# A hybrid retention and S5 layer: two small groups of matmuls are laid out on the array's four column groups, in full float

## The chip, the cores and the metric

The kernel runs on one core of one Trainium2 chip. The metric is the device time of one execution in microseconds; the median of three runs counts. A separate, profiled execution gives the rows that are shown: its span goes from the first to the last instruction, and its own time is 2.55 us longer than the span. Engines are named as in the profile: PE is TensorE (matmuls; PEld its loads of weights), DVE is VectorE, ACT is ScalarE, POOL is GpSimd, SP is SyncE, which issues DMAs.

## What is computed

One layer over 1,024 prompt tokens and 8 sample tokens (1,032 columns in all). The normalised input is projected by one wide matrix; the parts feed a retention branch of eight heads and an S5 branch of 64 groups; both are gated, projected, merged and projected again. Two pieces matter here. In retention, the sample rows need a product of the query with the new state, and a normalisation of the result over the head's 128 values:

```python
    q_dec = q * jnp.exp((idx[None, :] + 1.0) * lg[:, None])[None, :, :, None]
    cross = jnp.einsum('bhqd,bhdv->bhqv', q_dec, s0)
...
    mu = jnp.mean(o, axis=-1, keepdims=True)
    var = jnp.mean(jnp.square(o - mu), axis=-1, keepdims=True)
    o = (o - mu) * lax.rsqrt(var + EPS)
```

In S5, each group of 16 channels has a linear recurrence over 64 complex states:

```python
    y = (jnp.einsum('gnp,bcgp->bcgn', cr, xr) - jnp.einsum('gnp,bcgp->bcgn', ci, xi)
         + dsk[None, None] * u_c)
```

## The kernel before, in words

**The large products.** All wide matrices are multiplied by a scheme with seven products for each 2x2 block of tiles; `product` (L924) issues the matmuls of one. Each factor is split into a high and a low half (`fp32r`), and three of the four combinations are summed, so a product is a run of matmuls 256 and 260 columns wide (324 near the end) with weights `whia`, `whib`, `whic` (high) and `wloa`, `wlob`, `wloc` (low). ScalarE casts the high half (L905) and VectorE subtracts it for the low half (`sub`, shown as L85). These products fill TensorE from about 340 us on.

**The branches in between.** The S5 branch and retention are Python generators in a queue `bg`. After each product, `slot()` lets the first of them go on to its next `yield`, with its instructions placed behind the ones just issued. A scheduler then settles the order within each engine; the engines work off their lists in order. So small matmuls of the branches stand in TensorE's list between two products.

**S5.** The 64 groups are handled in 16 blocks of four. `s5_mats` builds `B1` (128 x 4 groups x 16) and `W3` (128 x 4 x 9 x 16); `s5_toep` forms a block's Toeplitz kernels: four float matmuls (L643), with 16 columns of weights each, write 16 partitions x 128 values, side by side along one PSUM bank (`misc`). VectorE copies the bank to `ksb` (L645) and adds the skip term to the first 16 columns, by a multiply of the identity with `dsk` (L647, `dti`) and an addition (L648). Four DMAs from POOL's queue (L650) lay `ksb` out in `t_d` in DRAM as a Toeplitz matrix, and one more (L653) brings it back as `Tm`, for `s5_read` (L720, L721) one block later.

**Retention.** `head` handles one head after the other, eight in all. For the sample rows, VectorE multiplies the new state `s0` by the query (L1141, tile `vT`, 128 x 8 samples x 128), and TensorE sums over the partitions: for each half of the samples, `split` makes a high and a low half in the tile `ktS` (ScalarE, then VectorE), and eight matmuls (L1149) with an 8-column selector `sel` add row b of an 8 x 128 result. The two halves are one `yield`, so one product, apart. The result goes to `ons` (8 x 128, L1153), is normalised with the prompt's chunks (L1165 to L1179, with powers on GpSimd, L1171 and L1172), and is transposed by an 8-row transpose (L1190) behind the last group of full transposes (L1185). `load_vk` (L1064) loads the next head's `vT` from POOL's queue.

PSUM in this stretch: three double banks `acc` for the products and two single banks `misc` for all the rest.

Of the kernel before, what the change touches and what calls it, by code (L numbers as in the profile page):

```python
# [48 lines left out]
def constants():  # L49
# [25 lines left out]
    c["sgn"] = sg  # L75
    c["sel"] = np.ascontiguousarray(np.broadcast_to(np.eye(8, dtype=f).reshape(1, 64), (128, 64)))
    return c


def emit(ctx, tc, I, O):  # L80
# [6 lines left out]
    def mul(out, a, b, eng=None):  # L87
        tt(out, a, b, ALU.mult, eng)
# [310 lines left out]
    def s5_params():  # L399
# [9 lines left out]
        A.dma_start(prm, I["prm"])  # L409
        dsk = s5q.tile([16, G], F32, name="dsk")  # L410
        A.dma_start(dsk, I["dsk"])
        pp["dsk"] = dsk
        lr, li, ld = prm[:, 0, :], prm[:, 1, :], prm[:, 2, :]
# [220 lines left out]
    def s5_toep(b):  # L634
        g0 = 4 * b
        pp = s5p
        d = s5d[b]
        B1, W3 = d["B1"], d["W3"]
        U = d["U"] = W("U", [128, 4, 144])
        P.dma_start(U, ub_d[g0 * 16:g0 * 16 + 64].rearrange("(g n) s c -> (n s) g c", g=4))  # L640
        ps = misc()
        for g in range(4):
            T.matmul(ps[0:16, g * 128:(g + 1) * 128], B1[:, g, :], W3[:, g, 0:8, :], start=True, stop=True)  # L643
# [395 lines left out]
    def ret_const():  # L1039
# [17 lines left out]
        V.tensor_copy(K["sel"], selr.rearrange("p (b c) -> p b c", b=8))  # L1057
        yield
# [10 lines left out]
    def head(h):  # L1069
# [74 lines left out]
        for i in range(2):  # L1144
            hl = R("ktS", [128, 2, 4, 128], 1, F32R)
            split((hl[:, 0], hl[:, 1]), pq[:, 4 * i:4 * i + 4])
            for b in range(4):
                for e in range(2):
                    T.matmul(ps[0:8, 0:128], sel[:, 4 * i + b, :], hl[:, e, b, :], start=i + b + e == 0, stop=i == 1 and b == 3 and e == 1)  # L1149
# [13 lines left out]
        if h != HEADS[-1]:  # L1163
            K["next"] = load_vk(HEADS[HEADS.index(h) + 1])
        V.bn_stats(bn[0:8, 8], ons)  # L1165
        V.bn_aggr(mv[0:8, 8], bn[0:8, 8])
# [3 lines left out]
        V.tensor_scalar(rs[0:8, 8:9], mv[0:8, 8, 1:2], EPS, None, ALU.add)  # L1170
        P.tensor_tensor(rs[:, 0:8], rs[:, 0:8], mhalf, ALU.pow)  # L1171
        P.tensor_tensor(rs[0:8, 8:9], rs[0:8, 8:9], mhalf[0:8, 0:1], ALU.pow)  # L1172
# [3 lines left out]
        V.scalar_tensor_tensor(nb[0:8, 8:9], mv[0:8, 8, 0:1], -1.0, rs[0:8, 8:9], ALU.mult, ALU.mult)  # L1176
        for n in range(8):
            A.activation(on[:, n], on[:, n], AF.Identity, scale=rs[:, n:n + 1], bias=nb[:, n:n + 1])
        A.activation(ons, ons, AF.Identity, scale=rs[0:8, 8:9], bias=nb[0:8, 8:9])  # L1179
        yield  # L1180
# [8 lines left out]
        ps = misc()  # L1189
        T.transpose(ps[:, 0:8], ons, ident[0:8, 0:8])  # L1190
        mul(oo[:, SEQ:TOK], ps[:, 0:8], za[:, SEQ:TOK])
        P.dma_start(ya_d[h], oo)
# [585 lines left out]
def layouts(i):  # L1778
# [39 lines left out]
    r["x0s"] = c(stack2(xr.transpose(2, 1, 0), xi.transpose(2, 1, 0)))  # L1818
    r["dsk"] = c(a["s5_d"][0].T)
    br, bi = (a[n][0].transpose(1, 0, 2) for n in ("s5_b_re", "s5_b_im"))  # L1820
# [31 lines left out]
```

## Time and profile before

| | us |
|---|---|
| median of three runs | 2562.95 (2561.0 to 2564.02) |
| profiled execution, own time | 2561.65 |
| its span | 2559.1 |
| TensorE busy in it | 2532.5 |
| VectorE / ScalarE / GpSimd busy | 1996.9 / 971.4 / 763.4 |

How to read the rows that follow. A row of the timeline has the start in us from the span's start, the length, the engine, the line, the operation, the tiles (written <- read), the size (for a matmul: rows * columns of weights, then the moving operand) and how many instructions were merged into it; idle time ahead of it stands in brackets, with what ended it. Starts are exact to some hundredths; lengths of matmuls overlap, since they are pipelined. A row of grouped instructions has its busy time and mean length behind the bar, then the idle time ahead. A row of stretches gives, for each engine, busy us and instructions, then TensorE's granted clock (1.00 is full), and DMA share and rate.

### The profile page before, as it was taken

To read this page: it belongs to the slowest core of one execution; us is meant where nothing else is said; L and a number is where in the kernel's file an instruction comes from. 1 tells how busy PE (TensorE), PEld (TensorE's weight loads), DVE (VectorE), ACT (ScalarE), POOL (GpSimd) and SP (SyncE) were. 2 spreads that over 40 slices of the span, in tenths; PEclk is the share of its full clock that TensorE was granted. 3 is DMA by queue.
4 is the path that set the end of the run, shared out by engine and by line. 5 is a ranking of instruction groups with operands and counts; after the bars stand their busy time and mean duration, and the time that the engine had idled before them with its cause. 6 is when DMAs were issued, how large, how long until landed. Compare 5 with 4: busy or idle time off the path is not lost.

```text
span 2559.1 us, 52524 instructions
## 1 busy us (share of the span) xinstructions
PE 2532.5 (99%) x19948; PEld 2486.0 (97%) x19948; DVE 1996.9 (78%) x4183; ACT 971.4 (38%) x1747; POOL 763.4 (30%) x1276
## 2 busy tenths in 40 slices
PE   9999999999999999999999999999999999999998
PEld 8999999999999999999999999999999999999876
DVE  7655988898898887557987667667897878989784
ACT  7113223333233334343334444444552432445532
POOL 0103222222222222333334444434332222433320
PEclk9999999999999999999999999999999999999999
DMA  5886434434444447887879888888888689857884
GB/s 196 262 264 216 156 122 123 134 122 132 129 123 127 124 128 245 199 215 198 209 191 246 231 218 227 202 225 236 275 287 281 222 236 316 296 188 168 212 297 134
DMA packets 233500, 519.09 MB, mean 203 GB/s; under 512 B 33968, under 2 KB 61056, under 8 KB 232480
## 3 DMA queue, kind: packets, MB, share of 16 engines
q0 software_dynamic: 103008, 301.75, 41.7%
q1 hardware_dynamic: 91552, 159.30, 19.8%
q10 hardware_dynamic: 38688, 54.70, 6.7%
q8 instruction: 157, 2.57, 0.4%
q14 instruction: 95, 0.78, 0.1%
HBM read 342.36 MB, written 173.25 MB: 201 GB/s over the span
## 4 chain that ended last, share of the span: by engine, by line
PE 90%; DVE 4%; issue 3%; DMA 2%; POOL 1%; ACT 1%; DVEq 0%; POOLq 0%; ACTq 0%
PE acc L924 71%; PE acc L1755 5%; PE mm L220 3%; PE mm L218 3%; PE mm L219 3%; DVE a L85 1%; PE misc L643 1%; PE misc L721 1%; PE misc L720 1%; PE misc L1135 1%; PE misc L1125 1%; PE misc L1104 1%; DVE u L85 1%; PE misc L671 1%; PE misc L1137 0%
## 5 line engine op out<-in xcount | busy, mean ns | idle before, releaser
L924 PE MATMUL acc<-a,whib 128*128 128x256 f32 (+1 forms) x3656 | 607.0, 285 | 2.3 <-DVE u L85 2.2
L924 PE MATMUL acc<-a,whia 128*128 128x256 f32 (+1 forms) x3656 | 607.2, 285 | 1.7 <-DVE u L85 1.2
L924 PE MATMUL acc<-a,whic 128*128 128x256 f32 (+1 forms) x3664 | 606.9, 285 | 1.2 <-ACT whib L905 0.6
L924 PEld LDWEIGHTS acc<-a,whib 128*128 128x128 f32 x3656 | 508.8, 188 | 6.5 <-ACT whia L905 2.4
L924 PEld LDWEIGHTS acc<-a,whia 128*128 128x128 f32 x3656 | 509.6, 188 | 3.2 <-issue 1.9
L924 PEld LDWEIGHTS acc<-a,whic 128*128 128x128 f32 x3664 | 507.3, 188 | 2.0 <-ACT whib L905 0.8
L924 PE MATMUL acc<-a,wloa 128*128 128x256 f32 (+2 forms) x1828 | 383.4, 284 | 0.0
L924 PE MATMUL acc<-a,wloc 128*128 128x256 f32 (+2 forms) x1832 | 382.8, 283 | 0.4 <-DVE wloc L85 0.4
L924 PE MATMUL acc<-a,wlob 128*128 128x256 f32 (+2 forms) x1828 | 382.8, 284 | 0.0
L924 PEld LDWEIGHTS acc<-a,wloc 128*128 128x128 f32 x1832 | 286.5, 188 | 1.2 <-DVE wloc L85 1.2
L924 PEld LDWEIGHTS acc<-a,wloa 128*128 128x128 f32 x1828 | 286.3, 188 | 0.0
L924 PEld LDWEIGHTS acc<-a,wlob 128*128 128x128 f32 x1828 | 286.0, 188 | 0.2
L905 ACT CAST whib<-wraw 128x512 fp32r<-128x512 f32 x140 | 87.0, 621 | 232.0 <-PE acc L924 181.5
L905 ACT CAST whia<-wraw 128x512 fp32r<-128x512 f32 x142 | 88.1, 620 | 226.8 <-PE acc L924 170.9
L905 ACT CAST whic<-wraw 128x512 fp32r<-128x512 f32 x142 | 88.1, 621 | 213.8 <-PE acc L924 163.2
L85 DVE TENSOR_TENSOR wloa<-wraw,whia 128x512 fp32r<-128x512 f32 x152 | 104.2, 686 | 64.0 <-ACT whia L905 37.3
L85 DVE TENSOR_TENSOR wlob<-wraw,whib 128x512 fp32r<-128x512 f32 x151 | 103.5, 685 | 59.1 <-ACT whib L905 39.4
L85 DVE TENSOR_TENSOR wraw<-wr 128x512 f32<-128x512 f32 x212 | 145.3, 686 | 2.6
L905 ACT CAST whib<-wr 128x512 fp32r<-128x512 f32 x107 | 66.4, 620 | 191.2 <-PE acc L924 169.1
L85 DVE TENSOR_TENSOR wloc<-wraw,whic 128x512 fp32r<-128x512 f32 x153 | 104.8, 685 | 43.8 <-ACT whic L905 29.2
L905 ACT CAST whic<-wr 128x512 fp32r<-128x512 f32 x106 | 65.7, 620 | 190.9 <-PE acc L924 167.8
L905 ACT CAST whia<-wr 128x512 fp32r<-128x512 f32 x105 | 65.1, 620 | 189.3 <-PE acc L924 172.1
(457 smaller groups left out, 4575.8 us busy)
## 6 DMA issues: line engine op xcount, KB each, us to landing
wr<-in_w_in SPq DMA_DIRECT2D x280, 256.0 KB
pt_d<-u POOLq DMA_DIRECT2D x70, 258.0 KB, 3.3
u<-pt_d POOLq DMA_DIRECT2D x70, 258.0 KB, 5.0
wr<-in_w_out SPq DMA_DIRECT2D x64, 256.0 KB
wr<-in_w_outB SPq DMA_DIRECT2D x64, 256.0 KB
stg<-fm_d POOLq DMA_DIRECT2D x44, 258.0 KB, 4.3
pt_d<-st POOLq DMA_DIRECT2D x35, 258.0 KB, 3.3
pt_d<-p POOLq DMA_DIRECT2D x35, 258.0 KB, 2.9
```

The costliest lines, as they stand in the source:

```text
L85: return (eng or V).tensor_tensor(out, a, b, op)
L218: T.matmul(ps, wh[:, i, :], xh[:, t0:t1], start=first, stop=False)
L219: T.matmul(ps, wh[:, i, :], xl[:, t0:t1], start=False, stop=False)
L220: anchor["p"] = T.matmul(ps, wl[:, i, :], xh[:, t0:t1], start=False, stop=last).ins
L643: T.matmul(ps[0:16, g * 128:(g + 1) * 128], B1[:, g, :], W3[:, g, 0:8, :], start=True, stop=True)
L671: T.matmul(ps[:, q * 144:(q + 1) * 144], W1[:, g, :], U[:, g, :], start=True, stop=True)
L720: T.matmul(o, Tm[:, g, :], U[:, g, 0:136], start=True, stop=False)
L721: T.matmul(o, W3[:, g, 1:9, :], X[:, g, 0:136], start=False, stop=True)
L905: anchor["a"] = A.copy(hi, f).ins
L924: anchor["p"] = T.matmul(o, a[:, i, :], x, start=first and i == 0 and a is wh and b is xh, stop=n in (2, 5, 6) and i == 3 and a is wl, ski ...
L1104: T.matmul(ps[:, c * 128:(c + 1) * 128], kt[:, 4 * i + c, :], vt[:, 4 * i + c, :], start=True, stop=True)
L1755: anchor["p"] = T.matmul(ps[c], a, b, start=k == 0 and a is xh and b is wh, stop=k == KD - 1 and a is xl).ins
```

## The change

Both small groups of matmuls get a place in the array (`tile_position`), so that four of them lie on the four groups of 32 columns, in plain float.

The Toeplitz kernel of group g of a block goes to columns 32g to 32g + 31, and so to those partitions of PSUM. Its weights are 32 columns (a pair of groups of `B1`), of whose results 16 rows are used. The bank is then 128 partitions x 128 values instead of 16 x 512; the skip term is added as the first 16 columns are copied, by one operation with two parameters laid out by partition, `dsk` and `eye`. The DMAs to `t_d` have the same sizes and read other partitions.

The sums for samples are taken from the float product itself (`pq`, in `vT`); `split` and its tile go. For each half i, sample 4i + b goes to column group b with a 32-column selector that puts it in row 32b + i. So there are two float matmuls for each column group, one in each half, and the result `ons` has 128 partitions, eight of them used. What handles it (L1153, L1165 to L1179) works on 128 partitions instead of 8; the transpose at the end is a full one, and its multiply picks the eight columns.

```diff
         ps = misc()
         for g in range(4):
-            T.matmul(ps[0:16, g * 128:(g + 1) * 128], B1[:, g, :], W3[:, g, 0:8, :], start=True, stop=True)
-        ksb = W("ksb", [16, 4, 128])
-        V.tensor_copy(ksb, ps[0:16, :].rearrange("p (g l) -> p g l", g=4))
-        dt_ = W("dti", [16, 4, 16])
-        mul(dt_, ident[0:16, 0:16].unsqueeze(1).broadcast_to([16, 4, 16]), pp["dsk"][:, g0:g0 + 4].unsqueeze(2).broadcast_to([16, 4, 16]))
-        add(ksb[:, :, 0:16], ksb[:, :, 0:16], dt_)
+            T.matmul(ps[32 * g:32 * g + 32, 0:128], B1[:, g & 2:(g & 2) + 2, :].rearrange("p g n -> p (g n)"), W3[:, g, 0:8, :],
+                     start=True, stop=True, tile_position=(0, 32 * g))
+        ksb = W("ksb", [128, 128])
+        V.tensor_copy(ksb[:, 16:128], ps[:, 16:128])
+        V.scalar_tensor_tensor(ksb[:, 0:16], pp["eye"], pp["dsk"][:, b:b + 1], ps[:, 0:16], ALU.mult, ALU.add)
         for g in range(4):
             P.dma_start(bass.AP(tensor=t_d.tensor, offset=t_d.offset + (g0 + g) * 32768, ap=[[2048, 16], [272, 8], [1, 128]]),
-                        ksb[:, g, :].unsqueeze(1).broadcast_to([16, 8, 128]))
+                        ksb[32 * g + 16 * (g % 2):32 * g + 16 * (g % 2) + 16].unsqueeze(1).broadcast_to([16, 8, 128]))
...
-        selr = rp.tile([128, 64], F32, name="selr")
-        P.dma_start(selr, I["sel"])
-        K["sel"] = rp.tile([128, 8, 8], F32R, name="sel")
+        K["sel"] = rp.tile([128, 2, 32], F32, name="sel")
+        P.dma_start(K["sel"].rearrange("p b c -> p (b c)"), I["sel"])
...
         ps = misc()
         for i in range(2):
-            hl = R("ktS", [128, 2, 4, 128], 1, F32R)
-            split((hl[:, 0], hl[:, 1]), pq[:, 4 * i:4 * i + 4])
             for b in range(4):
-                for e in range(2):
-                    T.matmul(ps[0:8, 0:128], sel[:, 4 * i + b, :], hl[:, e, b, :], start=i + b + e == 0, stop=i == 1 and b == 3 and e == 1)
+                T.matmul(ps[32 * b:32 * b + 32, 0:128], sel[:, i, :], pq[:, 4 * i + b], start=i == 0, stop=i == 1,
+                         tile_position=(0, 32 * b), skip_group_check=True)
             if i == 0:
                 yield
-        ons = R("ons", [8, 128])
-        A.copy(ons, ps[0:8, 0:128])
+        ons = R("ons", [128, 128])
+        A.copy(ons, ps[:, 0:128])
...
-        P.tensor_tensor(rs[0:8, 8:9], rs[0:8, 8:9], mhalf[0:8, 0:1], ALU.pow)
+        P.tensor_tensor(rs[:, 8:9], rs[:, 8:9], mhalf[:, 0:1], ALU.pow)
...
-        A.activation(ons, ons, AF.Identity, scale=rs[0:8, 8:9], bias=nb[0:8, 8:9])
+        A.activation(ons, ons, AF.Identity, scale=rs[:, 8:9], bias=nb[:, 8:9])
...
         ps = misc()
-        T.transpose(ps[:, 0:8], ons, ident[0:8, 0:8])
-        mul(oo[:, SEQ:TOK], ps[:, 0:8], za[:, SEQ:TOK])
+        T.transpose(ps[:, 0:128], ons, ident)
+        eb = lambda t: t.rearrange("p (e b) -> p e b", e=2)
+        mul(eb(oo[:, SEQ:TOK]), ps[:, 0:128].rearrange("p (b r) -> p r b", r=32)[:, 0:2], eb(za[:, SEQ:TOK]))
```

The order of TensorE's list, at the first sums of the first head; `ktS` holds the split halves, `vT` the product, `acc` the products' banks. Before:

```order
L924 MATMUL acc<-a_2173,wloc 128x256
L924 MATMUL acc<-a_2173,wloc 128x260
L1149 MATMUL misc<-ktS,sel 8x128
L924 MATMUL acc<-a_2233,whia 128x256
L1149 MATMUL misc<-ktS,sel 8x128 x7
L924 MATMUL acc<-a_2233,whia 128x260
```

The same place in the changed kernel, whose line numbers differ by a few:

```order
L923 MATMUL acc<-a_2173,wloc 128x256
L923 MATMUL acc<-a_2173,wloc 128x260
L1143 MATMUL misc<-vT,sel 32x128 x4
L923 MATMUL acc<-a_2233,whia 128x256
L923 MATMUL acc<-a_2233,whia 128x260
```

The eight matmuls with one product matmul among them became four that stand together, at the same place between the same products. The second group (eight, now four), the Toeplitz groups and the transposes also keep their places.

VectorE's list at the same place, from the product with the query on. Before:

```order
L85 TENSOR_TENSOR vT<-a_16965,a_16964 128x1024
L85 TENSOR_TENSOR wlob<-wraw,whib 128x512
L85 TENSOR_TENSOR wraw<-wr,wraw 128x512
L85 TENSOR_TENSOR wraw<-wr 128x512
L85 TENSOR_TENSOR ktS<-vT,ktS 128x512
L85 TENSOR_TENSOR u_17610<-p_17566,acc 128x516
```

And in the changed kernel:

```order
L85 TENSOR_TENSOR vT<-a_16935,a_16934 128x1024
L85 TENSOR_TENSOR wlob<-wraw,whib 128x512
L85 TENSOR_TENSOR wraw<-wr,wraw 128x512
L85 TENSOR_TENSOR wraw<-wr 128x512
L85 TENSOR_TENSOR u_17578<-p_17534,acc 128x516
```

The low half's subtraction, which TensorE's sums read, is gone, and they read what the first row writes.

More of the change, by code (lines that the diff above doesn't have):

```diff
@@ L75, in constants @@
     c["sgn"] = sg
-    c["sel"] = np.ascontiguousarray(np.broadcast_to(np.eye(8, dtype=f).reshape(1, 64), (128, 64)))
+    c["sel"] = np.ascontiguousarray(np.broadcast_to(np.eye(32, dtype=f)[0:2].reshape(1, 64), (128, 64)))
     return c
@@ L409, in s5_params @@
         A.dma_start(prm, I["prm"])
-        dsk = s5q.tile([16, G], F32, name="dsk")
-        A.dma_start(dsk, I["dsk"])
-        pp["dsk"] = dsk
+        for n in ("dsk", "eye"):
+            pp[n] = s5q.tile([128, 16], F32, name=n)
+            A.dma_start(pp[n], I[n])
         lr, li, ld = prm[:, 0, :], prm[:, 1, :], prm[:, 2, :]
@@ L1056, in ret_const @@
         yield
-        V.tensor_copy(K["sel"], selr.rearrange("p (b c) -> p b c", b=8))
         yield
@@ L1164, in head @@
             K["next"] = load_vk(HEADS[HEADS.index(h) + 1])
-        V.bn_stats(bn[0:8, 8], ons)
-        V.bn_aggr(mv[0:8, 8], bn[0:8, 8])
+        V.bn_stats(bn[:, 8], ons)
+        V.bn_aggr(mv[:, 8], bn[:, 8])
         rs = R("rsd", [128, 9])
@@ L1169, in head @@
         V.tensor_scalar(rs[:, 0:8], mv[:, 0:8, 1], col[:, 3, h:h + 1], EPS, ALU.mult, ALU.add)
-        V.tensor_scalar(rs[0:8, 8:9], mv[0:8, 8, 1:2], EPS, None, ALU.add)
+        V.tensor_scalar(rs[:, 8:9], mv[:, 8, 1:2], EPS, None, ALU.add)
         P.tensor_tensor(rs[:, 0:8], rs[:, 0:8], mhalf, ALU.pow)
-        P.tensor_tensor(rs[0:8, 8:9], rs[0:8, 8:9], mhalf[0:8, 0:1], ALU.pow)
+        P.tensor_tensor(rs[:, 8:9], rs[:, 8:9], mhalf[:, 0:1], ALU.pow)
         yield
@@ L1175, in head @@
         V.scalar_tensor_tensor(nb[:, 0:8], mv[:, 0:8, 0], -1.0, rs[:, 0:8], ALU.mult, ALU.mult)
[L1176 removed]
+        V.scalar_tensor_tensor(nb[:, 8:9], mv[:, 8, 0:1], -1.0, rs[:, 8:9], ALU.mult, ALU.mult)
         for n in range(8):
             A.activation(on[:, n], on[:, n], AF.Identity, scale=rs[:, n:n + 1], bias=nb[:, n:n + 1])
[L1179 removed]
+        A.activation(ons, ons, AF.Identity, scale=rs[:, 8:9], bias=nb[:, 8:9])
         yield
@@ L1818, in layouts @@
     r["x0s"] = c(stack2(xr.transpose(2, 1, 0), xi.transpose(2, 1, 0)))
-    r["dsk"] = c(a["s5_d"][0].T)
+    r["dsk"], r["eye"] = np.zeros((4, 32, 16), np.float32), np.zeros((4, 32, 16), np.float32)
+    for g in range(4):
+        rows = slice(16 * (g % 2), 16 * (g % 2) + 16)
+        r["dsk"][g, rows] = a["s5_d"][0].reshape(16, 4, 16)[:, g].T
+        r["eye"][g, rows] = np.eye(16, dtype=np.float32)
+    r["dsk"], r["eye"] = (r[n].reshape(128, 16) for n in ("dsk", "eye"))
     br, bi = (a[n][0].transpose(1, 0, 2) for n in ("s5_b_re", "s5_b_im"))
```

## The prediction

> **What bounds the kernel now.** I read the page first: which engine is busy, and what the chain that ended last is made of.
>
> ```profile
> PE 2532.5 (99%) x19948; PEld 2486.0 (97%) x19948; DVE 1996.9 (78%) x4183; ACT 971.4 (38%) x1747; POOL 763.4 (30%) x1276
> PE 90%; DVE 4%; issue 3%; DMA 2%; POOL 1%; ACT 1%; DVEq 0%; POOLq 0%; ACTq 0%
> ```
>
> Then I asked for the busy time of each engine in the two stretches that the change touches: 340 to 940 us, where the S5 branch is worked off between the products of the large matrices, and 1380 to 1770 us, where retention is.
>
> ```profile
> 340.00:940.00 600.00, 598.76 (x5009) 590.83 (x5008) 532.65 (x1419) 189.63 (x350) 162.85 (x289) 1.00 0.42 126
> 1380.00:1770.00 390.00, 388.62 (x3326) 382.69 (x3325) 265.65 (x598) 176.77 (x339) 160.39 (x236) 1.00 0.84 219
> ```
>
> The first busy figure is TensorE (PE): 598.76 of 600 us and 388.62 of 390. It rests for 1.2 and 1.4 us. So in both stretches TensorE time is kernel time: what a small matmul group takes out of the stream of products is what it costs, and work of the other engines counts only where TensorE waits for it. Busy time can't price a group, since matmuls overlap in it. I price by starts instead, from the timeline: the row ahead of a group, the group, and the rows behind it, until the stream runs at its own pace again. The pace, and one Toeplitz group (L643):
>
> ```profile
> 347.08 0.40 PE L924 MATMUL acc<-a,wloa 128*128 128x256 f32 x2
> 347.32 0.64 PE L924 MATMUL acc<-a,whia 128*128 128x256 f32 x4
> 347.79 0.40 PE L924 MATMUL acc<-a,wloa 128*128 128x256 f32 x2
> 348.12 1.05 PE L643 MATMUL misc<-W,B 128*16 128x128 f32 x8
> 349.10 0.74 PE L924 MATMUL acc<-a,whib 128*128 128x256 f32 x4
> 349.68 0.40 PE L924 MATMUL acc<-a,wlob 128*128 128x256 f32 x2
> ```
>
> Two products take 0.24 us (347.08 to 347.32) and four 0.47 (to 347.79). The group could start at 347.79 + 0.24 = 348.03, and the four products behind it would have begun at 349.68 - 0.47 = 349.21. So it costs 1.18 us. It is four matmuls, each shown as two passes (x8). A group of float matmuls over the full width of the array, for comparison (L1104):
>
> ```profile
> 1360.35 0.40 PE L924 MATMUL acc<-a,wloc 128*128 128x256 f32 x2
> 1360.59 1.05 PE L1104 MATMUL misc<-a,ktS 128*128 128x128 f32 x8
> 1361.40 0.73 PE L924 MATMUL acc<-a,whia 128*128 128x256 f32 x4
> 1361.96 0.40 PE L924 MATMUL acc<-a,wloa 128*128 128x256 f32 x2
> ```
>
> From 1360.35 + 0.24 to 1361.96 - 0.47 is 0.90 us for eight passes: 0.11 each. The 16-column group pays 0.28 us beyond that, half as it enters (348.12 against 348.03), the rest as it leaves. That is the toll for a narrow float group among full-width products. The Trainium skill (TensorEngine Tiling (Array Packing), Key Properties) says that a change of tiling mode drains TensorE; the 0.28 agrees.
>
> **The change, part by part.**
>
> *Toeplitz kernels, 16 blocks.* The toll stays: the groups are still narrow, and still stand between products. What changes is how the eight passes lie. Nothing in this trace shows two column groups at work at once, so I bound it: no overlap is eight passes in a row, 0.90 + 0.28 = 1.18; complete overlap is two passes, 0.22 + 0.28 = 0.50. I take a value between, from the order of the passes: in the timeline each matmul's two passes stand together (x8 in one row, issued matmul by matmul). If TensorE starts them strictly in order, the second pass of group 0 waits for the first on the same columns, group 1's first pass may run beside group 0's second, and so on: five steps instead of eight, 5 x 0.1125 = 0.56, with the toll 0.84 us. That saves 16 x (1.18 - 0.84) = 5.4 us. In the Trainium skill, TensorE: Matmul & The Clock Gate, Part 3, what overlaps and what doesn't, has matmuls strictly in order, in start and end; no run here shows it for column groups.
>
> *Retention's sums for samples, 8 heads.* Now, sixteen single-pass matmuls on split halves, in two groups; the first head's:
>
> ```profile
> 1384.37 0.40 PE L924 MATMUL acc<-a,wloc 128*128 128x256 f32 x2
> 1384.60 0.22 PE L1149 MATMUL misc<-ktS,sel 128*8 128x128 f32 x1
> 1385.17 0.58 PE L1149 MATMUL misc<-ktS,sel 128*8 128x128 f32 x7 [0.18 <-DVE ktS L85]
> 1386.01 0.40 PE L924 MATMUL acc<-a,wloa 128*128 128x256 f32 x2
> 1388.37 0.64 PE L1149 MATMUL misc<-ktS,sel 128*8 128x128 f32 x8
> 1388.85 0.69 PE L924 MATMUL acc<-a,whib 128*128 128x256 f32 x4
> 1389.38 0.40 PE L924 MATMUL acc<-a,wlob 128*128 128x256 f32 x2
> ```
>
> The first group costs 1386.01 - 0.47 - 1384.61 = 0.93 us, of which some 0.4 is TensorE waiting for the low half (ktS). The second costs 1389.38 - 0.47 - 1388.37 = 0.54. Passes are 0.06 each, and there is no toll at the start: these narrow groups are cheap already. In six of the eight heads the second group waits too; the first and last of the six:
>
> ```profile
> 1491.45 0.76 PE L1149 MATMUL misc<-ktS,sel 128*8 128x128 f32 x8
> 1492.05 0.68 PE L924 MATMUL acc<-a,whic 128*128 128x256 f32 x4
> 1749.64 0.74 PE L1149 MATMUL misc<-ktS,sel 128*8 128x128 f32 x8
> 1750.22 0.70 PE L924 MATMUL acc<-a,whia 128*128 128x256 f32 x4
> ```
>
> That is 0.60 and 0.58 to the next product, against 0.48 in the first head: 0.11 more, so a head costs 0.93 + 0.54 + 0.75 x 0.11 = 1.55 us. After: two groups per head, each of four float matmuls on four column groups, so each like a new Toeplitz group: 2 x 0.84 = 1.68. The waits go, since the sums read the product itself (vT), which is there long before:
>
> ```profile
> 1377.58 1.22 DVE L85 TENSOR_TENSOR vT<-a,a 128x1024 f32<-128x1024 f32 x1
> ```
>
> It ends at 1378.80, 5.8 us ahead of the sums. So this part loses 8 x (1.68 - 1.55) = 1.0 us: the waits saved don't quite pay for two tolls.
>
> *The transpose of the sample rows, 8 heads.* The group of four full transposes (L1185), alone and with the 8-row transpose (L1190) behind it:
>
> ```profile
> 1397.17 0.40 PE L924 MATMUL acc<-a,wloa 128*128 128x256 f32 x2
> 1397.41 0.60 PE L1185 MATMUL misc<-ident,kT 128*128 128x128 f32 x4
> 1398.32 0.40 PE L924 MATMUL acc<-a,wlob 128*128 128x256 f32 x2
> 1400.45 0.40 PE L924 MATMUL acc<-a,wlob 128*128 128x256 f32 x2
> 1401.22 0.22 PE L1190 MATMUL misc<-ident,ons 8*128 8x8 f32 x1
> 1401.96 0.40 PE L924 MATMUL acc<-a,wloc 128*128 128x256 f32 x2
> ```
>
> Alone: 1398.32 - 0.47 - 1397.41 = 0.44 us, 0.11 each. With L1190: 1401.96 - 0.47 - 1400.69 = 0.80. So the small transpose costs 0.36, a toll again. Made full-width it becomes a fifth transpose at 0.11: 8 x 0.25 = 2.0 us saved, whatever the column groups do.
>
> *Beside the path.* The evacuation on VectorE (16x512 copy, 0.68 us, and two small operations) becomes a 128x112 copy and a 128x16 operation. By free size they lie below the 128x128 read of PSUM here:
>
> ```profile
> L1111 DVE SCALAR_TENSOR_TENSOR a<-a,misc 128x128 f32<-128x128 f32 x56 | 15.8, 282 | 0.8
> L85 DVE TENSOR_TENSOR ktS<-vT,ktS 128x512 fp32r<-128x512 f32 x16 | 10.9, 683 | 0.0
> L1735 POOL TENSOR_TENSOR small<-small x3: 548/553/578, 2542.9 to 2551.9; 128x1 f32<-128x1 f32 x3
> ```
>
> The sixteen low halves (second row) and as many casts on ScalarE go. Neither engine bounds, so beyond the waits counted above this is nothing. The power on 128x1 instead of 8x1 costs no more: 0.55 us (third row) against this:
>
> ```profile
> 1393.64 0.63 POOL L1172 TENSOR_TENSOR rsd<-rsd,mhalf 8x1 f32<-8x1 f32 x1
> 1395.45 3.19 ACT L1178 ACTIVATE kT<-kT,nb,rsd 128x128 f32<-128x128 f32 x8
> 1388.47 0.54 POOL L1064 DMA_DIRECT2D vT<-v_d  x1 [0.15 <-issue]
> ```
>
> That matters: it stands ahead of the scaling of kT (second row), whose first four end near 1397.05, only 0.36 us before the transposes at 1397.41. Longer by more than that, it would stall TensorE. One wait is added: the load of the next head's vT (third row, in POOL's queue) must now let TensorE finish the second sums. At 0.84 us from 1388.37 that is 1389.2, 0.7 later; behind it in POOL's queue stand loads that have products of slack, so I cost it at nothing. The t_d writes keep count and size; one more parameter load on ScalarE's queue, once, lies in its 62% of free time.
>
> **Sum.** -5.4 + 1.0 - 2.0 = -6.4 us. The profiled execution took 2561.65 us (span 2559.1, 2.55 around it), 1.3 below the median of 2562.95. Taken off the median: 2556.5 us.
>
> **The rivals.** All hang on one length, x, of a narrow float group of eight passes; the sum is 16(x - 1.18) + 8(2x - 1.55) - 2.0, zero at x = 1.04 us. A measurement of this kernel can tell about 0.2%, 5.1 us: that is x under 0.88 or over 1.20.
>
> *Full overlap:* the passes queue up for each column group and all groups run at once, x = 0.50. That gives -10.9 - 4.4 - 2.0 = -17.3, 2545.6 us. For it: the passes of different groups share no columns. Against: they are issued in order, two by two. The Trainium skill (TensorEngine Tiling (Array Packing), Theoretical Speedup) promises up to 4x for 32 columns, which would be this.
>
> *Groups don't overlap:* the change doesn't do what it says, x = 1.18. Toeplitz gains nothing, retention loses 8 x 0.81 = 6.5, the transposes give 2.0: +4.5, 2567.5 us. For it: no overlap of narrow groups in this trace, though L643 and L1149 stay on one column group, so they could show none.
>
> *Slower, weight loads in the open:* now the load for the next pass hides behind the running one.
>
> ```profile
> L643 PEld LDWEIGHTS misc<-W,B x128: 92/97/97, 348.1 to 931.1; 128*16 128x16 f32 x128
> ```
>
> If the load for another column group must wait until the running pass is out of the array, three loads of 0.097 us lie open in each group and no passes overlap: x = 1.18 + 0.29 = 1.47. Then +4.6 + 11.1 - 2.0 = +13.7, 2576.7 us; it decides once x passes 1.04. Against: with one column group the loads do hide. The Trainium skill, TensorE: Matmul & The Clock Gate, Part 3, lets a load overlap running matmuls only where the row group differs, and these four share all rows: it speaks for this rival; no run here shows it.
>
> **How the numbers follow.** Forecast (x = 0.84) 0.42, full overlap 0.30, no overlap 0.16, open loads 0.08, some new wait or luck of the order 0.04. The forecast lies 1.3 us past the 0.2% bound; I give two thirds of it to faster. Faster: 0.30 + 0.28 + 0.01 = 0.59. Within 0.2%: 0.14 + 0.10 (no overlap, +4.5) + 0.02 = 0.26. Slower: 0.06 + 0.08 + 0.01 = 0.15. The range reaches from full overlap to no overlap, 2545.5 to 2568; open loads and the last case stay outside.
>
> **What would show it.** In the timeline after, from the Toeplitz row's start to the next product (0.98 us now, 0.20 of the 1.18 lying outside): 0.64 for the forecast, 0.30 for full overlap, 0.98 for none, 1.27 for open loads. Both groups of sums in a head should look like it, without a wait for VectorE. Five transposes in a row should run at one pace. I am wrong if the two stretches shorten by other than about 5 us and 1 us, or if TensorE gains idle time there.

## The result, and the profile after

The changed kernel took 2546.09 us (median of four runs, 2545.13 to 2547.11) against 2562.34 us for the kernel before (four runs, 2561.0 to 2564.02): a ratio of 0.9933, with a 95% interval of 0.992 to 0.9945. The forecast was 2556.5 us. The direction was right, but the change gained more than double what the sum of -6.4 us said. The profiled spans are 2543.5 us and 2559.1 us, so 15.6 us apart, and the working below is made against this 15.6.

First the page of the changed kernel, its engine totals and the chain that ended last:

```profile
PE 2520.0 (99%) x19948; PEld 2473.5 (97%) x19948; DVE 1976.3 (78%) x4150; ACT 962.7 (38%) x1731; POOL 763.0 (30%) x1276
PE 90%; DVE 3%; issue 3%; DMA 2%; POOL 1%; ACT 0%; DVEq 0%; POOLq 0%; ACTq 0%; SPq 0%
```

TensorE still runs 99% of the span and still carries 90% of the chain, with the same number of matmul records (19948). VectorE has lost 20.6 us of work (1996.9 before), which lies beside the path. The two stretches, the S5 branch and retention:

```profile
340.00:940.00 600.00, 598.94 (x5099) 592.94 (x5098) 532.14 (x1424) 192.12 (x354) 164.31 (x293) 1.00 0.41 128
1370.00:1750.00 380.00, 380.00 (x3285) 373.38 (x3284) 253.08 (x576) 165.31 (x319) 158.92 (x235) 1.00 0.85 221
```

TensorE is idle for 1.1 us of the first and for none of the second. In the same 600 us it starts 5099 matmul passes instead of 5009. So the premise of the prediction held (in these stretches TensorE time is kernel time), no new wait came in, and the gain must show in the length of the small groups. One Toeplitz group (L643) in the timeline:

```profile
348.85 0.40 PE L923 MATMUL acc<-a,wloa 128*128 128x256 f32 x2
349.18 0.43 PE L643 MATMUL misc<-W,B 128*32 128x128 f32 x8
349.53 0.75 PE L923 MATMUL acc<-a,whib 128*128 128x256 f32 x4
350.12 0.40 PE L923 MATMUL acc<-a,wlob 128*128 128x256 f32 x2
```

From its start to the next product it takes 349.53 - 349.18 = 0.35 us, where the prediction had listed 0.64 for the forecast, 0.30 for full overlap, 0.98 for none and 1.27 for open weight loads. By starts, as in the prediction, it costs 350.12 - 0.47 - (348.85 + 0.24) = 0.56 us; the mean over the 16 groups is 0.546, against 1.170 before. Now the first sums of the first head, and then its second:

```profile
1375.08 0.43 PE L1143 MATMUL misc<-vT,sel 128*32 128x128 f32 x8
1375.44 0.74 PE L923 MATMUL acc<-a,whia 128*128 128x256 f32 x4
...
1378.47 0.42 PE L1143 MATMUL misc<-vT,sel 128*32 128x128 f32 x8
1378.83 0.74 PE L923 MATMUL acc<-a,whib 128*128 128x256 f32 x4
```

Both take 0.36 us to the next product, with no wait: the same thing as a Toeplitz group (mean of the 16: 0.549). A head costs 1.10 us instead of 1.55. The full transposes (L1180) with the one of the sample rows (L1185) behind them:

```profile
1390.80 0.60 PE L1180 MATMUL misc<-ident,kT 128*128 128x128 f32 x4
...
1391.82 0.40 PE L923 MATMUL acc<-a,wloc 128*128 128x256 f32 x2
```

Five transposes cost 1391.82 - 0.47 - 1390.80 = 0.55 us, 0.11 each, as forecast. The sum measured is 16 x (0.546 - 1.170) + 8 x (1.10 - 1.55) + 8 x (0.55 - 0.80) = -10.0 - 3.6 - 2.0 = -15.6 us, the difference of the two spans. That it meets this difference to a tenth is chance: two more profiles of the changed kernel, taken later, have spans of 2547.1 and 2547.4 us.

A length that is free of what happens before and behind these parts runs from the first Toeplitz group to the last sample transpose. These two rows, of the view by line, give first and last starts in the kernel before:

```profile
L643 PE MATMUL misc<-W,B x128: 272/273/284, 348.1 to 931.3; 128*16 128x128 f32 x128
L1190 PE MATMUL misc<-ident,ons x8: 223/224/225, 1401.2 to 1762.7; 8*128 8x8 f32 x8
```

and these in the changed kernel:

```profile
L643 PE MATMUL misc<-W,B x128: 272/285/297, 349.2 to 921.7; 128*32 128x128 f32 x128
L1185 PE MATMUL misc<-ident,ons x8: 272/273/273, 1391.2 to 1748.0; 128*128 128x128 f32 x8
```

From 348.1 to 1762.7 it was 1414.6 us, from 349.2 to 1748.0 it is 1398.8: 15.8 less. Of this 10.7 lie between the first and the last Toeplitz group (583.2 us before, 572.5 after): 10.0 are the groups, and the rest goes with waits of the products for VectorE's sums in the same time, of which there were, before and after:

```profile
PE acc L924 <- DVE u L85: 1.2, 4, 0.4
```

```profile
PE acc L923 <- DVE u L85: 0.8, 2, 0.4
```

The columns are us in total, count and longest. I call the length from the first Toeplitz group to the last sample transpose **the distance** from here on; each row of the table below is one profile, and the same kernel profiled again comes within 0.15 us of it (the changed one three times, one with a single group of sums twice), where the timed medians of the changed kernel differed by 3 us.

Were the passes really started together, or is each only shorter? The timeline cut to the group's first 70 ns (the window 349.17 to 349.25) says:

```profile
349.18 0.32 PE L643 MATMUL misc<-W,B 128*32 128x128 f32 x4
```

Four of the eight passes start in there. Busy time in short windows, for this line alone (columns: the window, its length, then PE and PEld busy with the count of instructions that run in it):

```profile
349.25:349.29 0.04, 0.04 (x4) 0.04 (x8) 1.00 0.00 0
349.29:349.35 0.06, 0.06 (x8) 0.04 (x6) 1.00 0.00 0
```

Four passes still run until 349.29, and then the other four join them. In the trace's records the steps from start to start are 7, 6, 7, 113, 7, 7 and 6 ns, with 203 ns to the next product. So in this group the four column groups each run one pass at once, and 0.11 us later each its second. The starts show it; the ends of the passes are modelled by the profile. The clock is 1.00 in all these rows.

### The profile page after: what moved, and what is told of

The parts are those of the page before. It is cut to its first block, busy times and chain, and to the rows that moved or that the text cites. A ratio compares the mean times of both kernels' runs of the same rounds, so it can differ in the third digit from the quotient of the medians.

```text
span 2543.5 us, 52483 instructions
## 1 busy us (share of the span) xinstructions
PE 2520.0 (99%) x19948; PEld 2473.5 (97%) x19948; DVE 1976.3 (78%) x4150; ACT 962.7 (38%) x1731; POOL 763.0 (30%) x1276
## 4 chain that ended last, share of the span: by engine, by line
PE 90%; DVE 3%; issue 3%; DMA 2%; POOL 1%; ACT 0%; DVEq 0%; POOLq 0%; ACTq 0%; SPq 0%
PE acc L923 72%; PE acc L1751 4%; PE mm L220 3%; PE mm L218 3%; PE mm L219 3%; DVE a L85 1%; PE misc L719 1%; PE misc L720 1%; PE misc L670 1%; PE misc L1132 1%; PE misc L1122 1%; PE misc L1101 1%; PE misc L1134 0%; DVE u L85 0%; DMA xr<-in_xT 0%
## 5 line engine op out<-in xcount | busy, mean ns | idle before, releaser
L923 PE MATMUL acc<-a,whia 128*128 128x256 f32 (+1 forms) x3656 | 606.8, 285 | 1.6 <-DVE u L85 0.8
L923 PE MATMUL acc<-a,whib 128*128 128x256 f32 (+1 forms) x3656 | 606.6, 285 | 1.4 <-ACT a L265 1.3
L923 PE MATMUL acc<-a,whic 128*128 128x256 f32 (+1 forms) x3664 | 606.7, 285 | 1.2 <-ACT whib L904 0.6
L923 PEld LDWEIGHTS acc<-a,whib 128*128 128x128 f32 x3656 | 508.7, 188 | 6.1 <-issue 2.6
L923 PEld LDWEIGHTS acc<-a,whia 128*128 128x128 f32 x3656 | 509.7, 188 | 3.7 <-issue 2.7
L923 PEld LDWEIGHTS acc<-a,whic 128*128 128x128 f32 x3664 | 507.2, 188 | 3.0 <-issue 1.0
L923 PE MATMUL acc<-a,wloa 128*128 128x256 f32 (+2 forms) x1828 | 383.4, 284 | 0.0
L923 PE MATMUL acc<-a,wloc 128*128 128x256 f32 (+2 forms) x1832 | 382.8, 283 | 0.4 <-DVE wloc L85 0.4
L923 PE MATMUL acc<-a,wlob 128*128 128x256 f32 (+2 forms) x1828 | 382.9, 284 | 0.0
L923 PEld LDWEIGHTS acc<-a,wloc 128*128 128x128 f32 x1832 | 286.6, 188 | 1.2 <-DVE wloc L85 1.2
L923 PEld LDWEIGHTS acc<-a,wloa 128*128 128x128 f32 x1828 | 286.3, 188 | 0.0
L923 PEld LDWEIGHTS acc<-a,wlob 128*128 128x128 f32 x1828 | 286.0, 188 | 0.2
```

Of the source, the lines that this page charges most:

```text
L923: anchor["p"] = T.matmul(o, a[:, i, :], x, start=first and i == 0 and a is wh and b is xh, stop=n in (2, 5, 6) and i == 3 and a is wl, ski ...
```

## The experiments

All were timed against the kernel before on the same chip. In the last column is the distance of each, from the first and last starts in its trace.

| kernel | median us | before beside it | ratio, 95% interval | distance us |
|---|---|---|---|---|
| before | - | - | - | 1414.6 |
| changed | 2546.09 | 2562.34 | 0.9933, 0.992 to 0.9945 | 1398.8 |
| Toeplitz groups alone | 2551.52 | 2562.76 | 0.9956, 0.9944 to 0.9969 | 1403.9 |
| full transpose alone | 2560.42 | 2562.76 | 0.999, 0.9981 to 0.9999 | 1413.0 |
| old sums, split earlier | 2548.22 | 2562.76 | 0.9942, 0.993 to 0.9955 | 1400.4 |
| one group of eight sums | 2545.08 | 2562.76 | 0.9929, 0.9916 to 0.9943 | 1397.9 |
| two column groups, in turn | 2549.3 | 2564.4 | 0.994, 0.9925 to 0.9955 | 1400.5 |
| two column groups, in runs | 2548.87 | 2564.4 | 0.9937, 0.9922 to 0.9952 | 1400.6 |
| one group of sums, in runs | 2545.78 | 2564.4 | 0.993, 0.9913 to 0.9946 | 1398.0 |
| changed, again | 2548.09 | 2562.56 | 0.9942, 0.9928 to 0.9955 | 1398.8 |
| one group of eight, again | 2547.42 | 2562.56 | 0.9938, 0.9925 to 0.995 | 1398.0 |
| one group, one power | 2543.82 | 2563.07 | 0.9923, 0.9909 to 0.9936 | 1396.6 |
| changed, third time | 2549.11 | 2563.07 | 0.9941, 0.9929 to 0.9954 | 1398.8 |

### The parts alone

**The Toeplitz groups alone.** The S5 part of the diff is kept; the sums and their transpose are those of the kernel before.

> The kernel before with the new Toeplitz groups alone; the sums for samples and their transpose stay as they were. If the column groups work at the same time (a group costs 0.55 us where it cost 1.18), 16 x 0.63 = 10.1 us come off the kernel before: ratio 0.9961. If the list's order held them to five steps as I had forecast, 5.4 us: ratio 0.9979, and most of the 16 us would come from elsewhere, from the freed VectorE and ScalarE for one.

Measured: 11.2 us faster, by the medians. Its groups cost 0.546 us, to the third place the same as in the changed kernel, and the distance is 10.7 us shorter. The 16 groups give 10.0 of these, as in the changed kernel.

**The full transpose alone.** Everything else is that of the kernel before; the normalised rows are held in a tile of 128 partitions whose other rows are zeros.

```diff
-        T.transpose(ps[:, 0:8], ons, ident[0:8, 0:8])
+        T.transpose(ps[:, 0:128], ons, ident)
```

> The kernel before with the full-width transpose of the sample rows alone (the unused rows are zeroed by GpSimd). If the 8-row transpose pays the toll of a narrow group and the full one does not, 8 x 0.25 = 2.0 us come off: ratio 0.9992. If the toll moves to somewhere else, or the zeroing holds up the list, nothing comes off (1.0000).

Measured: 2.3 us faster, its interval just clear of 1; the distance, in which seven of the eight transposes lie whole, is 1.6 us shorter (by the forecast, 7 x 0.25 = 1.75). In its timeline, the five transposes from the first to the products behind them:

```profile
1401.51 0.60 PE L1186 MATMUL misc<-ident,kT 128*128 128x128 f32 x4
...
1402.54 0.40 PE L924 MATMUL acc<-a,wloc 128*128 128x256 f32 x2
```

1402.54 - 0.47 - 1401.51 = 0.56 us, against 0.80. This term of the sum is shown by itself. What the column groups do in retention is then the difference of the changed kernel from the two parts: 15.8 - 10.7 - 1.6 = 3.5 us of the distance.

### Where retention's gain comes from

**The old sums, split earlier.** The split halves and the sixteen narrow matmuls (L1152 here) are kept, with the new Toeplitz groups and the full transpose; but each half is split one product before its matmuls, so that they need not wait for it.

```diff
+        def halves(i):
+            hl = R("ktS", [128, 2, 4, 128], 1, F32R)
+            split((hl[:, 0], hl[:, 1]), pq[:, 4 * i:4 * i + 4])
+            return hl
+        hl = halves(0)
...
             if i == 0:
                 yield
+                hl = halves(1)
```

> New Toeplitz groups, the full-width transpose, and the old sums from split halves on one set of columns, but with each half split one product earlier, so that TensorE should not wait for it. If what the new sums gained is only the waits, an old group costs 0.53 us without them, a new one 0.55, and this kernel is as fast as the changed one, some 16 us under the kernel before (ratio 0.9937). If laying the sums on four column groups is itself a gain, this one stays 2 to 4 us behind the changed kernel (ratio 0.9945 to 0.9953).

The first group of the first head has no wait any more:

```profile
1375.18 0.65 PE L1152 MATMUL misc<-ktS,sel 128*8 128x128 f32 x8
1375.66 0.70 PE L923 MATMUL acc<-a,whia 128*128 128x256 f32 x4
1376.19 0.40 PE L923 MATMUL acc<-a,wloa 128*128 128x256 f32 x2
...
1480.40 0.22 PE L1152 MATMUL misc<-ktS,sel 128*8 128x128 f32 x1
1480.79 0.59 PE L1152 MATMUL misc<-ktS,sel 128*8 128x128 f32 x7 [0.17 <-DVE ktS L85]
1481.22 0.68 PE L923 MATMUL acc<-a,whic 128*128 128x256 f32 x4
```

1376.19 - 0.47 - 1375.18 = 0.54 us, the price of eight passes of 0.06 and nothing more. A new group costs 0.549. So where the old group doesn't wait, the new one is no cheaper. The gain of the new sums over the old ones is the waits, as the later head shows: there the second group still waits, since VectorE has the half ready late. From 1480.40 to 1481.22 is 0.82 us, against 0.48 in the first head. The waits for VectorE, all heads:

```profile
PE misc L1152 <- DVE ktS L85: 1.1, 6, 0.2
```

Six waits of up to 0.2 us, and the groups that wait cost 0.86 to 0.89 us by starts; over the 16 groups the mean is 0.66. The distance is 1.6 us longer than in the changed kernel, near 16 x (0.66 - 0.55) = 1.8. My expectation that an earlier split alone would remove the waits held for the first groups and failed for six of the eight second ones. In retention, then, the new groups are no shorter than the old ones without their waits. What gains is that the sums read the product directly: no split, no wait. The column groups are what lets float sums do so at this price: eight float passes on one column group cost 1.17 us in the Toeplitz groups of before, and two such groups for each head would be 2.34 us, more than the old 1.55. That is an estimate; no run has float sums on one column group.

### How the passes are started

Two theories were left for why the passes overlap. Either each column group has passes waiting of its own, so that the order in the program doesn't matter; or TensorE looks only a pass or two past a blocked one, so that it matters which stands next. In the changed kernel successive matmuls lie on different column groups, and both say the same. So I put the four Toeplitz matmuls on two column groups only, once in turn and once two and two. (The copy to `ksb` and the skip term are laid out to suit, for 64 partitions.)

**Two column groups, in turn.**

```diff
-        for g in range(4):
-            T.matmul(ps[32 * g:32 * g + 32, 0:128], ...
-                     start=True, stop=True, tile_position=(0, 32 * g))
+        for g in (0, 1, 2, 3):
+            e, c = g % 2, 128 * (g // 2)
+            T.matmul(ps[32 * e:32 * e + 32, c:c + 128], ...
+                     start=True, stop=True, tile_position=(0, 32 * e))
```

> The changed kernel, but the four Toeplitz matmuls of a block lie on two column groups instead of four, issued in turn (0, 1, 0, 1); their results take two halves of the bank. If each column group works off its own passes, four stand in a row on each: 0.44 us and the toll of 0.33, so 0.77 us for a group instead of 0.55, and 16 x 0.22 = 3.5 us on top of the changed kernel (ratio to the kernel before 0.995). If passes started strictly in the list's order, as I had forecast, five steps: 0.89 us, 5.4 us on top.

**Two column groups, in runs.** The same with another order, so that four passes of column group 0 stand ahead of the first one of group 1.

```diff
-        for g in (0, 1, 2, 3):
+        for g in (0, 2, 1, 3):
```

> The same with the matmuls of one column group issued together (0, 0, 1, 1). If a column group can queue up all of its passes, the order is nothing to it: 0.77 us again. If it can hold one pass beside the running one, the list stands still while group 0 works off two of its four, and group 1 starts 0.22 us late: 0.99 us, 7 us on top of the changed kernel. If strictly in order, seven steps: 1.11 us, 9 us on top.

The group in turn:

```profile
349.11 0.63 PE L644 MATMUL misc<-W,B 128*32 128x128 f32 x8
349.67 0.74 PE L925 MATMUL acc<-a,whib 128*128 128x256 f32 x4
```

and in runs:

```profile
349.03 0.64 PE L644 MATMUL misc<-W,B 128*32 128x128 f32 x8
349.60 0.74 PE L925 MATMUL acc<-a,whib 128*128 128x256 f32 x4
```

0.56 and 0.57 us to the next product; by starts 0.759 and 0.763, four steps of passes and the toll, and one distance for both (1400.5 and 1400.6). The order makes no difference. The kernel in runs, in the 80 ns from 349.02 to 349.10, starts two passes:

```profile
349.03 0.31 PE L644 MATMUL misc<-W,B 128*32 128x128 f32 x2
```

In the records the second of them comes 14 ns after the first, then 120 ns pass, and so on in pairs (14, 120, 13, 96, 13, 96, 13). A second pass on the same columns comes 0.11 us after the first (the step in the changed kernel), so the pass at 14 ns is the other group's. Four passes stand ahead of it in the program, of which one had started: it overtook three. That the two orders reached TensorE as they were written is seen in the same steps: in turn, the second pass of each pair comes 6 or 7 ns after the first, not 13 or 14. Strict order falls (it would make 1.11 us), and so does the short look ahead (0.99). Both kernels come out at 2549.3 and 2548.87 us. Against the changed kernel their groups are 16 x 0.21 = 3.4 us dearer, but the distance is only 1.7 us longer. Of the 1.7 us between, 1.1 are the changed kernel's two waits for VectorE's sums `u` (the row `PE acc L923 <- DVE u` above): 0.4 us each in the profile, 0.56 and 0.54 with the restart by the steps between starts, and absent from the traces of these two kernels. So a shorter group gives some of its gain back where VectorE is late. The last 0.6 us stay open.

### One toll for each group

**One group of eight sums.** Both halves stand in one group, and the `yield` comes behind it. Each column group then has two matmuls, four passes, and there is one group for each head instead of two.

```diff
-            if i == 0:
-                yield
+        yield
```

> The changed kernel with both halves of the sums in one group: eight float matmuls together, two per column group, so four passes in a row on each: 0.44 us and one toll of 0.33 instead of twice 0.22 + 0.33. If the toll is paid once per group and the column groups run side by side, 8 x (1.10 - 0.77) = 2.6 us come off the changed kernel, and the ratio to the kernel before is 0.9927. If there is no toll per group, only a cost per pass, nothing comes off (0.9937).

```profile
1374.60 0.39 PE L923 MATMUL acc<-a,wloc 128*128 128x256 f32 x2
1374.92 0.64 PE L1143 MATMUL misc<-vT,sel 128*32 128x128 f32 x16
1375.49 0.74 PE L923 MATMUL acc<-a,whia 128*128 128x256 f32 x4
1376.07 0.40 PE L923 MATMUL acc<-a,wloa 128*128 128x256 f32 x2
```

1376.07 - 0.47 - (1374.60 + 0.24) = 0.76 us; the mean is 0.765. Sixteen passes cost 0.77 where two groups of eight cost 1.10: the difference, 0.33, is one toll, and four steps of 0.11 with a toll of 0.33 make 0.77. So the toll is paid for each group and not for each matmul, and a group of eight passes is 0.22 + 0.33 = 0.55. The distance, though, is only 0.9 us shorter than in the changed kernel, not 8 x 0.33 = 2.6.

**The same, two matmuls of a column group together** (the loops over `b` and `i` change places).

> The kernel with all sums of a head in one group, but the two matmuls of one column group issued together, one column group after the other. If a column group can queue up all of its passes: as before this edit, 0.77 us for a group of eight. If it holds one pass beside the running one, each column group starts 0.22 us after the one before: 0.66 + 0.44 + 0.33 = 1.43 us, 8 x 0.67 = 5.3 us more than issued in turn, about 2550.5 us.

```profile
1374.53 0.67 PE L1143 MATMUL misc<-vT,sel 128*32 128x128 f32 x16
1375.12 0.74 PE L923 MATMUL acc<-a,whia 128*128 128x256 f32 x4
```

0.59 us to the next product, 0.785 by starts. A short look ahead would have made 1.43. With four passes of one column group listed together, the steps between column groups are 13 ns instead of 7, and that is the 0.02.

**Changed kernel and one group, again,** to see whether the missing 1.7 us is noise.

> The changed kernel itself, on one chip with the next one, as a measure for it: some 16.3 us under the kernel before, ratio 0.9936.

> The changed kernel with both halves of the sums in one group, again, now beside the changed kernel. Its groups cost 0.77 us a head where two cost 1.10: 8 x 0.33 = 2.7 us less than the changed kernel if that difference reaches the end, ratio to the kernel before 0.9926. If something else takes its place at the end, the two are equal.

2548.09 and 2547.42: 0.7 us apart, with intervals that overlap, and 0.8 apart in the distance. So it isn't noise; part of the saving is lost in retention. The first head shows where, from the power on GpSimd over the scaling on ScalarE to the transposes, first in the changed kernel:

```profile
1381.66 1.69 POOL L1166 TENSOR_TENSOR rsd<-rsd,mhalf 128x8 f32<-128x8 f32 x1 [0.66 <-DVE rsd L1165]
1385.28 3.20 ACT L1173 ACTIVATE kT<-kT,nb,rsd 128x128 f32<-128x128 f32 x8
1387.27 0.60 PE L1180 MATMUL misc<-ident,kT 128*128 128x128 f32 x4
1387.62 0.72 PE L923 MATMUL acc<-a,whib 128*128 128x256 f32 x4
```

and then with one group, with two rows of VectorE ahead:

```profile
1381.66 0.68 DVE L85 TENSOR_TENSOR u<-acc,p 128x516 f32<-128x516 f32 x1
1382.26 0.22 DVE L1163 TENSOR_SCALAR rsd<-mv,col 128x8 f32<-128x8 f32 x1
1382.57 2.12 POOL L1165 TENSOR_TENSOR rsd<-rsd,mhalf 128x8 f32<-128x8 f32 x1 [0.75 <-DVE rsd L1164]
1386.43 3.19 ACT L1172 ACTIVATE kT<-kT,nb,rsd 128x128 f32<-128x128 f32 x8
1387.02 1.43 PE L1179 MATMUL misc<-ident,kT 128*128 128x128 f32 x4
1388.21 0.72 PE L923 MATMUL acc<-a,whib 128*128 128x256 f32 x4
```

With one group, VectorE's list has a sum of 0.68 us (`u`) ahead of the operation that GpSimd's power waits for (L1163); in the changed kernel that sum comes behind it. So the power starts 0.91 us later, takes 2.12 us instead of 1.69, and the scaling of kT starts 1.15 us later. The first group of transposes, whose matmuls need the scaled kT one by one, lasts 1.19 us instead of 0.35: 0.84 lost in the first head, and about as much in the second, together 1.7. In the other six heads the sum stays behind L1163, as in the changed kernel, and the first transposes last 0.35 us. Why the power itself takes longer in these two heads isn't shown. The view by line of the transposes names what TensorE sat idle for (us, times):

```profile
  ACT kT L1172: 1.5, 6
```

This is the chain of which the prediction said that it has only 0.36 us to spare. That was too little, since it let the first transpose wait for four scaled blocks, where each needs only its own: the scaling of kT begins 1.99 us ahead of the transposes in the changed kernel and 0.59 with one group, 1.40 less, and 0.84 of this was lost, so some 0.56 was to spare. In the changed kernel the chain held; a small move of VectorE's list breaks it.

**One group, one power.** To shorten that chain, the power over the eight prompt columns and the one over the sample column become one of nine columns, and so does the small product behind it.

```diff
-        K["mhalf"] = rp.tile([128, 8], F32, name="mhalf")
+        K["mhalf"] = rp.tile([128, 9], F32, name="mhalf")
...
-        P.tensor_tensor(rs[:, 0:8], rs[:, 0:8], mhalf, ALU.pow)
-        P.tensor_tensor(rs[:, 8:9], rs[:, 8:9], mhalf[:, 0:1], ALU.pow)
+        P.tensor_tensor(rs, rs, mhalf, ALU.pow)
...
-        V.scalar_tensor_tensor(nb[:, 0:8], mv[:, 0:8, 0], -1.0, rs[:, 0:8], ALU.mult, ALU.mult)
-        V.scalar_tensor_tensor(nb[:, 8:9], mv[:, 8, 0:1], -1.0, rs[:, 8:9], ALU.mult, ALU.mult)
+        V.scalar_tensor_tensor(nb, mv[:, :, 0], -1.0, rs, ALU.mult, ALU.mult)
```

> One group of sums per head, and one power and one bias over all nine columns instead of two each, now that the sample rows fill all partitions; ScalarE can then scale kT before ons. In the kernel with one group, TensorE waited 0.84 us for the scaled kT in each of the first two heads, since the chain through VectorE, GpSimd and ScalarE had no more than 0.36 us to spare. If that wait ate the saving, it goes, and 8 x 0.33 = 2.7 us come off the changed kernel: ratio to the kernel before 0.993 or a little less on this chip. If the saving is lost elsewhere, it stays level with the changed kernel.

> The changed kernel, as a measure for the run beside it: 15 to 16 us under the kernel before, ratio 0.9935 to 0.9942.

```profile
1387.46 0.88 PE L1177 MATMUL misc<-ident,kT 128*128 128x128 f32 x4
1388.09 0.72 PE L923 MATMUL acc<-a,whib 128*128 128x256 f32 x4
```

The first transposes last 0.63 us, so 0.28 of wait is left of 0.84; in the second head 0.32 is left. The distance is 2.2 us shorter than in the changed kernel (1396.6 against 1398.8), close to the 2.6 of the tolls less these two waits. The medians are 2543.82 and 2549.11, but their intervals overlap (0.9909 to 0.9936 and 0.9929 to 0.9954), and the total moves by more than the distance from run to run. It is the fastest kernel that was run, faster than the one before by 0.6 to 0.9%; that it beats the changed one rests on the distance, not on the total.

## Why the prediction was wrong in size

**The step that failed** is "If TensorE starts them strictly in order, the second pass of group 0 waits for the first on the same columns, group 1's first pass may run beside group 0's second, and so on: five steps instead of eight". The condition doesn't hold. The four first passes start within 20 ns and the four second ones 0.11 us later: two steps, not five. By the sign that the prediction set itself, about 5 us and 1 us off the two stretches, it is wrong as well: the first gave 10.7 us of the distance and the second 5.1. The rival of full overlap was the right mechanism; no overlap (0.98 from start to next product) and open weight loads (1.27) fall with the 0.35 measured. The runs on two column groups show that order in the program has no part in it.

**The length x** was forecast as 0.84 us and came out as 0.55. Full overlap had 0.50; the passes are as in that rival (0.22), but the toll is 0.33 instead of 0.28. It was taken from one group with sixteen columns, and the run with one group of eight sums gives it for groups on all four column groups. Of it, 0.09 lies ahead of the first pass (349.18 against 348.85 + 0.24). The old group, too, had 0.09 of its 0.28 there (348.12 against 348.03): a third, not the half that the prediction reads.

**Toeplitz:** -5.4 forecast, -10.0 measured (-11.2 by the run alone). The miss is x.

**Sums:** +1.0 forecast, -3.6 measured; with x = 0.55 the prediction's own formula gives 8 x (1.10 - 1.55) = -3.6. The old price was right (0.93 + 0.62 for a head), and so was "these narrow groups are cheap already": the early split showed that they are as cheap as the new ones where they don't wait. "The waits saved don't quite pay for two tolls" failed only through x: the old path's waits, 1.55 - 2 x 0.53 = 0.49 us in a head, are more than the whole gain of 0.45, and the overlap of the passes pays for the two tolls.

**Transposes:** -2.0 forecast, -2.0 by starts, -2.3 in the run alone. Right, and for the reason given.

**What was costed at nothing.** The load of the next head's `vT` now waits for the second sums:

```profile
1379.23 0.54 POOL L1061 DMA_DIRECT2D vT<-v_d  x1 [0.69 <-PE misc L1143]
```

The wait is there, 0.69 us in the first head; the load starts 1379.23 - 1378.47 = 0.76 after the second sums, and TensorE has no idle time there: costing it at nothing was right. The power on the column of 128 partitions (L1167):

```profile
L1167 POOL TENSOR_TENSOR rsd<-rsd,mhalf 128x1 f32<-128x1 f32 x8 | 5.5, 686 | 0.0
```

and the one on 8 partitions in the kernel before (L1172):

```profile
L1172 POOL TENSOR_TENSOR rsd<-rsd,mhalf 8x1 f32<-8x1 f32 x8 | 6.0, 746 | 0.0
```

The new one takes 686 ns in the mean where the narrow one took 746; the 0.63 us that the prediction shows is one of the shorter ones. So it costs no more, as was said, and no wait of TensorE came of it.

**The two pages that spoke against it.** The Trainium skill, TensorE: Matmul & The Clock Gate, Part 3, What overlaps and what doesn't, has matmuls strictly in order, in start and end, and lets a load of weights overlap running matmuls only where the row group differs. By the first I chose x = 0.84; this case's traces differ from both, and the measurement decides. In the changed kernel itself the four matmuls, counted by their first passes, may still start in their order; the run with two column groups in runs shows a pass that starts at 14 ns, ahead of three listed before it and not yet started. And eight loads for four column groups, which share all rows, lie within 0.16 us, beside passes that are running:

```profile
349.17 0.16 PEld L643 LDWEIGHTS misc<-W,B 128*32 128x32 f32 x8
```

The "up to 4x" of the Trainium skill (TensorEngine Tiling (Array Packing), Theoretical Speedup), which I had put with the rival, agrees for the passes: 8 x 0.11 = 0.87 us became 0.22. With the toll, the group went from 1.17 to 0.55, 2.1 times.

**The chances.** Full overlap had 0.30 against 0.42 for the forecast. What spoke against it, order of issue, was a rule and not a row; the trace of before could show neither. Where nothing in the trace speaks to a mechanism, its bounds deserve more than a point between them.

**What stays open:** what the toll is made of. By the starts of one Toeplitz group, 0.09 us of it lies ahead of the first pass and 0.09 behind the last (203 ns to the next product, where a pass takes 109), and 0.11 in the first product behind (225 ns to the next start, against 118 in the stream); the last 0.04 are passes that start a little late (153 ns from the first start to the last, where one step takes 109). What TensorE does in these times no trace shows. Open, too, are why narrow groups of split halves (`fp32r`, L1149) pay none, and how many passes can wait behind a running one beyond the three that were seen.

## What to carry to other kernels

Small float matmuls that would each use a strip of 32 columns belong on the array's four column groups, all of them in one group between the products: here their passes ran at once in each order that was tried, and the cost was one toll (0.33 us) plus two passes of 0.11 us for each matmul of a column group. Before crediting such a layout, look at what the old group cost without its waits: in retention the new groups were no shorter (0.55 against 0.53 us), and the gain was the split that they made needless. And after every such move look again at the chains with little to spare (here kT's scaling, some 0.56 us): merging the two groups of sums shifted VectorE's list, and that chain took back 1.7 of the 2.6 us.

## What the runs showed of the hardware that was not expected

Passes of float matmuls on different column groups start 7 ns apart when successive matmuls lie on different groups, and 13 to 14 ns apart when two matmuls of one group are listed together. A pass overtook three that are listed ahead of it on another column group and had not started. A group of narrow float matmuls among full-width products pays 0.33 us once, be it eight passes or sixteen; an 8-row transpose behind full ones cost 0.25 us more than a full one. And the length of TensorE's work between two fixed points repeated to 0.15 us between profiles, where medians of the changed kernel differed by 3 us (2546.09, 2548.09 and 2549.11): a change of 1 us is seen there and not in the total.
